# Rotary embedding on one core: rotation in three VectorE operations, and two rows of batch 0 stored early in float32

## The chip, the cores and the metric

The kernel runs on one core of a Trainium2 chip. The metric is device time in microseconds (us), taken from start to end of one execution; lower is better. Runs carry a state (fast or slow); every timed run quoted here is a fast one.

## The reference

The kernel applies a rotary embedding. Each row of 64 numbers is split into two halves of 32, which are rotated against each other by tables of cos and sin that depend on the sequence position only.

```python
# x: (8, 2048, 16, 64) float32; cos, sin: (2048, 32) float32
x1 = x[..., :32]; x2 = x[..., 32:]
out1 = x1 * cos - x2 * sin
out2 = x1 * sin + x2 * cos
return np.concatenate([out1, out2], axis=-1)
```

The input is 67.1 MB and so is the output. There are four multiplications for every pair of numbers moved, so the first thing to ask of any change is whether it moves fewer bytes.

## The kernel before

Each of the 8 batches is one tile `xt` of 128 partitions by 16,384 elements in float16 (16 positions `j`, 16 heads, 64 numbers). GpSimd issues the loads, which cast float32 to float16 on the way, and the stores, which cast back. There are five `xt` buffers. The two tables and the first two positions of batch 0 (`head`) come in float32 through SyncE and are cast on ScalarE.

```python
def rotate(xt):
    v = tmp_pool.tile([P, J, H, D], f16)
    # [...] sin_b, neg_b, cos_b: the float16 tables, broadcast over the heads
    nc.vector.tensor_mul(out=v[:, :, :, 0:Dh], in0=xt[:, :, :, Dh:D], in1=neg_b)   # -x2*sin
    nc.vector.tensor_mul(out=v[:, :, :, Dh:D], in0=xt[:, :, :, 0:Dh], in1=sin_b)   #  x1*sin
    # [...]
    nc.vector.tensor_mul(out=xw, in0=xw, in1=cos_b)                                #  x*cos, in place
    nc.vector.tensor_add(out=xa, in0=xa, in1=v...)                                 #  sum, in place

tiles = [load(b) for b in range(NBUF)]        # five loads issued at the start
# [...] ScalarE: head -> tiles[0], then the tables to float16
for b in range(B):
    rotate(tiles[b])
    if b < B - 1:
        store(b, tiles[b])
    if b + NBUF < B:
        tiles.append(load(b + NBUF))
# [...] the last batch goes out in three parts, the last two positions of it
#       cast by ScalarE and stored in float32 through SyncE
```

## Time and profile before

| | kernel before |
|---|---|
| time, median of 6 runs | 317.51 us (317.43 to 317.98) |
| span of the profiled execution | 315.6 us |
| VectorE busy | 209.2 us, 66% |
| DMA queues' share of 16 engines' span | 98.0% (GpSimd's) and 2.2% (SyncE's) |
| HBM traffic | 67.63 MB read, 67.11 MB written |

First come lines of the page of the kernel before: the span, VectorE's busy time, the DMA busy share in 40 equal slices (tenths, 9 is 90% or more), the two DMA queues, the HBM total, and the first line of the chain of work that ended last (followed back from the last instruction, at each step to what released it). In the profile DVE is VectorE, ACT ScalarE, POOL GpSimd and SP SyncE.

```profile
span 315.6 us, 126 instructions
...
DVE 209.2 (66%) x32; ACT 6.8 (2%) x6; POOL 9.4 (3%) x21
...
DMA  9899999999999999999999999999999999999998
...
q0 software_dynamic: 2448, 99.09, 98.0%
q1 hardware_dynamic: 576, 2.62, 2.2%
HBM read 67.63 MB, written 67.11 MB: 427 GB/s over the span
...
issue 25%; DMA 23%; DVE 21%; another core or an unknown queue 13%; POOL 1%; ACT 1%; SPq 0%; POOLq 0%; DVEq 0%; ACTq 0%
```

The reader should see two things. The DMA engines are at 9 tenths in nearly every slice, and the total, 134.7 MB in 315.6 us, is 427 GB/s. The chain line, on the other hand, gives VectorE 21% of the span, and "issue", time in which the engine waited for nothing that the profile shows, even more. Read alone it suggests that VectorE is worth working on.

Next are groups of VectorE instructions of the kernel before, with shapes kept apart: line, operation, operands, count, then busy us and mean ns of one, then the idle time before them.

```profile
L72 DVE TENSOR_TENSOR xt<-xt,v 128x16384 f16<-128x16384 f16 x8 | 69.5, 8692 | 0.3
L70 DVE TENSOR_TENSOR xt<-xt,cos_h 128x16384 f16<-128x16384 f16 x8 | 69.5, 8692 | 4.2 <-ACT cos_h L81 3.9
L67 DVE TENSOR_TENSOR v<-xt,neg_h 128x8192 f16<-128x8192 f16 x8 | 35.4, 4425 | 50.1 <-DMA xt<-in_x_dram 49.9
L68 DVE TENSOR_TENSOR v<-xt,sin_h 128x8192 f16<-128x8192 f16 x8 | 35.3, 4417 | 0.0
```

The four operations of a batch take 4.42 + 4.42 + 8.69 + 8.69 = 26.2 us. From the two sizes an operation costs about 0.15 us plus 0.52 us for a thousand elements.

Then the timeline of the kernel before: start, duration, instruction, and in brackets what it had waited for. Line 58 issues a store, line 51 a load.

```profile
23.51 4.43 DVE L67 TENSOR_TENSOR v<-xt,neg_h 128x8192 f16<-128x8192 f16 x1 [23.51 <-DMA xt<-in_x_dram]
27.85 4.42 DVE L68 TENSOR_TENSOR v<-xt,sin_h 128x8192 f16<-128x8192 f16 x1
35.55 0.62 ACT L81 CAST cos_h<-cos_f 128x512 f16<-128x512 f32 x1 [17.98 <-DMA cos_f<-in_cos_dram]
36.20 8.69 DVE L70 TENSOR_TENSOR xt<-xt,cos_h 128x16384 f16<-128x16384 f16 x1 [3.93 <-ACT cos_h L81]
...
54.18 0.54 POOL L58 DMA_DIRECT2D out_dram<-xt  x1 [50.14 <-DVE xt L72]
...
121.83 0.53 POOL L51 DMA_DIRECT2D xt<-in_x_dram  x1 [41.14 <-DMA out_dram<-xt]
...
141.13 0.53 POOL L51 DMA_DIRECT2D xt<-in_x_dram  x1 [18.76 <-DMA out_dram<-xt]
...
237.47 4.42 DVE L67 TENSOR_TENSOR v<-xt,neg_h 128x8192 f16<-128x8192 f16 x1 [24.82 <-DMA xt<-in_x_dram]
```

These lines give the transfer rate a second time. Load 5 was issued when store 0 had landed (121.8 us) and load 6 when store 1 had landed (141.1 us), so the one store between them, 8.39 MB, took 19.3 us. Eight loads and eight stores of this size make nearly the whole span. The lines also show how early VectorE is: the first store was issued at 54.2 us and had to wait in the queue behind five loads.

### The profile page before, as it was taken

To read this page: it belongs to the slowest core of one execution; us is meant where nothing else is said; L and a number is where in the kernel's file an instruction comes from. 1 tells how busy PE (TensorE), PEld (TensorE's weight loads), DVE (VectorE), ACT (ScalarE), POOL (GpSimd) and SP (SyncE) were. 2 spreads that over 40 slices of the span, in tenths; PEclk is the share of its full clock that TensorE was granted. 3 is DMA by queue.
4 is the path that set the end of the run, shared out by engine and by line. 5 is a ranking of instruction groups with operands and counts; after the bars stand their busy time and mean duration, and the time that the engine had idled before them with its cause. 6 is when DMAs were issued, how large, how long until landed. Compare 5 with 4: busy or idle time off the path is not lost.

```text
span 315.6 us, 126 instructions
## 1 busy us (share of the span) xinstructions
DVE 209.2 (66%) x32; ACT 6.8 (2%) x6; POOL 9.4 (3%) x21
## 2 busy tenths in 40 slices
DVE  0009599999999999999979999990009994000000
ACT  4010000000000000000000000000000002000000
POOL 3000000000000000010000000100000001000000
DMA  9899999999999999999999999999999999999998
GB/s 278 184 261 207 200 249 216 199 199 249 216 199 266 399 424 507 399 332 233 233 199 199 390 407 399 399 532 266 199 224 507 399 399 498 432 399 399 432 424 341
DMA packets 3024, 101.71 MB, mean 322 GB/s; under 512 B 336, under 2 KB 336, under 8 KB 592
## 3 DMA queue, kind: packets, MB, share of 16 engines
q0 software_dynamic: 2448, 99.09, 98.0%
q1 hardware_dynamic: 576, 2.62, 2.2%
HBM read 67.63 MB, written 67.11 MB: 427 GB/s over the span
## 4 chain that ended last, share of the span: by engine, by line
issue 25%; DMA 23%; DVE 21%; another core or an unknown queue 13%; POOL 1%; ACT 1%; SPq 0%; POOLq 0%; DVEq 0%; ACTq 0%
DMA xt<-in_x_dram 12%; DMA cos_f<-in_cos_dram 11%; DVE xt L70 8%; DVE xt L72 8%; DVE v L68 3%; DVE v L67 1%; ACT head L105 1%; POOL out_dram L58 1%; POOL xt L51 0%; ACT cos_h L81 0%; SPq L45 0%; SPq L36 0%; POOLq L58 0%; DVEq L67 0%
## 5 line engine op out<-in xcount | busy, mean ns | idle before, releaser
L70 DVE TENSOR_TENSOR xt<-xt,cos_h 128x16384 f16<-128x16384 f16 x8 | 69.5, 8692 | 4.2 <-ACT cos_h L81 3.9
L72 DVE TENSOR_TENSOR xt<-xt,v 128x16384 f16<-128x16384 f16 x8 | 69.5, 8692 | 0.3
L67 DVE TENSOR_TENSOR v<-xt,neg_h 128x8192 f16<-128x8192 f16 x8 | 35.4, 4425 | 50.1 <-DMA xt<-in_x_dram 49.9
L68 DVE TENSOR_TENSOR v<-xt,sin_h 128x8192 f16<-128x8192 f16 x8 | 35.3, 4417 | 0.0
L51 POOL DMA_DIRECT2D xt<-in_x_dram x8 | 4.4, 560 | 117.1 <-DMA out_dram<-xt 116.3
L105 ACT CAST head<-xt 128x2048 f32<-128x2048 f16 x1 | 1.9, 1897 | 227.6 <-DVE xt L72 227.6
L58 POOL DMA_DIRECT2D out_dram<-xt x7 | 3.7, 535 | 87.8 <-DVE xt L72 87.8
L95 POOL DMA_DIRECT2D out_dram<-xt x1 | 0.5, 531 | 50.5 <-DVE xt L72 50.5
L75 ACT CAST xt<-head 128x2048 f16<-128x2048 f32 x1 | 1.9, 1898 | 3.4 <-DMA head<-in_x_dram 3.4
L75 ACT ACT_TABLE_LOAD x1 | 1.3, 1283 | 0.7 <-PEq L127 0.7
L81 ACT CAST cos_h<-cos_f 128x512 f16<-128x512 f32 x1 | 0.6, 617 | 18.0 <-DMA cos_f<-in_cos_dram 18.0
L79 ACT CAST sin_h<-sin_f 128x512 f16<-128x512 f32 x1 | 0.6, 617 | 9.1 <-DMA sin_f<-in_sin_dram 9.1
L80 ACT ACTIVATE neg_h<-sin_f 128x512 f16<-128x512 f32 x1 | 0.6, 624 | 0.0
L97 POOL DMA_DIRECT2D out_dram<-xt x1 | 0.5, 531 | 0.0
L127 POOL MEMSET const-float32-0.0<- 128x1 f32 x1 | 0.1, 98 | 0.2 <-issue 0.2
L127 POOL MEMSET const-bfloat16-1.0<- 128x1 bf16 x1 | 0.1, 101 | 0.0
L127 POOL MEMSET const-float32-1.0<- 128x1 f32 x1 | 0.1, 98 | 0.0
L127 POOL MEMSET const-uint8-127<- 128x1 uint8 x1 | 0.1, 98 | 0.0
## 6 DMA issues: line engine op xcount, KB each, us to landing
xt<-in_x_dram POOLq DMA_DIRECT2D x7, 4096.0 KB, 41.1
out_dram<-xt POOLq DMA_DIRECT2D x1, 4608.0 KB, 42.3
xt<-in_x_dram POOLq DMA_DIRECT2D x1, 3584.0 KB, 22.2
out_dram<-xt POOLq DMA_DIRECT2D x1, 2560.0 KB, 47.9
head<-in_x_dram SPq DMA_DIRECT2D x1, 1024.0 KB, 4.7
out_dram<-head SPq DMA_DIRECT2D x1, 1024.0 KB, 8.4
sin_f<-in_sin_dram SPq DMA_DIRECT2D x1, 256.0 KB, 15.2
cos_f<-in_cos_dram SPq DMA_DIRECT2D x1, 256.0 KB, 33.9
```

The lines of the kernel that those rows point to most:

```text
L51: nc.gpsimd.dma_start(out=xt[:, j0:J, :, :].rearrange("p j h d -> p (j h d)"), in_=x[b].rearrange("(p j) h d -> p j (h d)", j=J)[:, j0:J, ...
L58: nc.gpsimd.dma_start(out=out[b].rearrange("(p j) h d -> p (j h d)", j=J), in_=xt)
L67: nc.vector.tensor_mul(out=v[:, :, :, 0:Dh], in0=xt[:, :, :, Dh:D], in1=neg_b)
L68: nc.vector.tensor_mul(out=v[:, :, :, Dh:D], in0=xt[:, :, :, 0:Dh], in1=sin_b)
L70: nc.vector.tensor_mul(out=xw, in0=xw, in1=cos_b)
L72: nc.vector.tensor_add(out=xa, in0=xa, in1=v.rearrange("p j h d -> p (j h d)"))
L75: nc.scalar.copy(out=tiles[0][:, 0:JA, :, :].rearrange("p j h d -> p (j h d)"), in_=head.rearrange("p j h d -> p (j h d)"),)
L79: nc.scalar.copy(out=sin_h, in_=sin_f)
L80: nc.scalar.mul(out=neg_h, in_=sin_f, mul=-1.0)
L81: nc.scalar.copy(out=cos_h, in_=cos_f)
L95: gate = nc.gpsimd.dma_start(out=dst, in_=src)
L105: nc.scalar.copy(out=head.rearrange("p j h d -> p (j h d)"), in_=src)
```

## The change

It has two parts. The two half multiplies become one, which reads the two halves of each row in swapped order against a table that holds minus sin and sin side by side. And the two positions of batch 0 that SyncE loads are rotated on their own, cast to float32 by ScalarE and stored through SyncE early, so that GpSimd's store of batch 0 is 1 MB smaller. The intent is less VectorE work and an earlier start of storing.

```diff
-    sin_h = const_pool.tile([P, J, Dh], f16)
-    neg_h = const_pool.tile([P, J, Dh], f16)
+    sin_h = const_pool.tile([P, J, D], f16)
[...]
-    def rotate(xt):
+    def rotate(xt, j0, j1):
[...]
-        nc.vector.tensor_mul(out=v[:, :, :, 0:Dh], in0=xt[:, :, :, Dh:D], in1=neg_b)
-        nc.vector.tensor_mul(out=v[:, :, :, Dh:D], in0=xt[:, :, :, 0:Dh], in1=sin_b)
+        xe = xt[:, js, :, :].rearrange("p j h (e d) -> p j h e d", e=2)
+        nc.vector.tensor_mul(
+            out=v[:, js, :, :].rearrange("p j h (e d) -> p j h e d", e=2),
+            in0=xe[:, :, :, ::-1, :],
+            in1=sin_b,
+        )
[...]
-    nc.scalar.copy(out=sin_h, in_=sin_f)
-    nc.scalar.mul(out=neg_h, in_=sin_f, mul=-1.0)
+    nc.scalar.copy(out=sin_h[:, :, Dh:D], in_=sin_f)
+    nc.scalar.mul(out=sin_h[:, :, 0:Dh], in_=sin_f, mul=-1.0)
     nc.scalar.copy(out=cos_h, in_=cos_f)
+    rotate(tiles[0], 0, JA)
+    nc.scalar.copy(out=head..., in_=tiles[0][:, 0:JA, :, :]...)
+    nc.sync.dma_start(out=out[0]...[:, 0:JA, :]..., in_=head...)
[...]
-        rotate(tiles[b])
+        rotate(tiles[b], JA if b == 0 else 0, J)
```

GpSimd's store of batch 0 leaves the first two positions out.

More of the change, by code (lines that the diff above doesn't have):

```diff
@@ L57, in store @@
     def store(b, xt):
+        j0 = JA if b == 0 else 0
         nc.gpsimd.dma_start(
-            out=out[b].rearrange("(p j) h d -> p (j h d)", j=J), in_=xt
+            out=out[b].rearrange("(p j) h d -> p j (h d)", j=J)[:, j0:J, :].rearrange("p j f -> p (j f)"),
+            in_=xt[:, j0:J, :, :].rearrange("p j h d -> p (j h d)"),
         )
-    def rotate(xt):
+    def rotate(xt, j0, j1):
         v = tmp_pool.tile([P, J, H, D], f16)
-        sin_b = sin_h.unsqueeze(2).to_broadcast([P, J, H, Dh])
-        neg_b = neg_h.unsqueeze(2).to_broadcast([P, J, H, Dh])
-        cos_b = cos_h.unsqueeze(2).to_broadcast([P, J, 2 * H, Dh])
-        nc.vector.tensor_mul(out=v[:, :, :, 0:Dh], in0=xt[:, :, :, Dh:D], in1=neg_b)
-        nc.vector.tensor_mul(out=v[:, :, :, Dh:D], in0=xt[:, :, :, 0:Dh], in1=sin_b)
-        xw = xt.rearrange("p j h (e d) -> p j (h e) d", d=Dh)
+        n = j1 - j0
+        js = slice(j0, j1)
+        shape = [P, n, H, 2, Dh]
+        sin_b = sin_h[:, js, :].rearrange("p j (e d) -> p j e d", e=2).unsqueeze(2).to_broadcast(shape)
+        cos_b = cos_h[:, js, :].unsqueeze(2).to_broadcast([P, n, 2 * H, Dh])
+        xe = xt[:, js, :, :].rearrange("p j h (e d) -> p j h e d", e=2)
[4 more added lines that the diff above has]
+        )
+        xw = xt[:, js, :, :].rearrange("p j h (e d) -> p j (h e) d", d=Dh)
         nc.vector.tensor_mul(out=xw, in0=xw, in1=cos_b)
-        xa = xt.rearrange("p j h d -> p (j h d)")
-        nc.vector.tensor_add(out=xa, in0=xa, in1=v.rearrange("p j h d -> p (j h d)"))
+        xa = xt[:, js, :, :].rearrange("p j h d -> p (j h d)")
+        nc.vector.tensor_add(out=xa, in0=xa, in1=v[:, js, :, :].rearrange("p j h d -> p (j h d)"))
     tiles = [load(b) for b in range(NBUF)]
@@ L78 @@
     )
-    nc.scalar.copy(out=sin_h, in_=sin_f)
-    nc.scalar.mul(out=neg_h, in_=sin_f, mul=-1.0)
+    nc.scalar.copy(out=sin_h[:, :, Dh:D], in_=sin_f)
+    nc.scalar.mul(out=sin_h[:, :, 0:Dh], in_=sin_f, mul=-1.0)
     nc.scalar.copy(out=cos_h, in_=cos_f)
+    rotate(tiles[0], 0, JA)
+    nc.scalar.copy(
+        out=head.rearrange("p j h d -> p (j h d)"),
+        in_=tiles[0][:, 0:JA, :, :].rearrange("p j h d -> p (j h d)"),
+    )
+    nc.sync.dma_start(
+        out=out[0].rearrange("(p j) h d -> p j (h d)", j=J)[:, 0:JA, :].rearrange("p j f -> p (j f)"),
+        in_=head.rearrange("p j h d -> p (j h d)"),
+    )
     def part(b, j0, j1):
```

## The prediction

> **What bounds the kernel now.** The DMA engines do. The page's slices give DMA 9 tenths nearly throughout, the queue table gives the GpSimd queue 98.0% and the SyncE queue 2.2% of 16 engines' span; VectorE is busy 66%. HBM traffic is 67.63 + 67.11 MB, 427 GB/s over the 315.6 us span. The waits confirm the rate: store 0 landed at 121.8, store 1 at 141.1, so 8.39 MB took 19.3 us; load 5 landed at 160.2, store 2 at 199.1, load 7 at 237.4: 38.2 to 38.9 us per pair. The Trainium skill ("DMA: Bandwidth & Descriptors", Specifications) states a fabric ceiling of 435 GB/s; the trace agrees within 2%. At that rate 134.7 MB need 310 us, so there is nearly nothing to win without moving fewer bytes.
>
> **What the change does.**
> 1. The two half multiplies (4.425 + 4.417 us) become one over 16,384 elements that reads the halves swapped. Innermost step stays 1 and the type float16; the skill ("Vector Engine (DVE) Microarchitecture Reference", table of perf-mode triggers) looks only at the innermost step. So I expect the 8.69 us of the other 16,384-element operations: 0.15 us saved a batch. The page lists negative steps as not measured; no run shows it yet.
> 2. Batch 0 is split: three operations over 2,048 elements (estimate from 8.69 us for 16,384 and 4.42 for 8,192: 1.2 us each) and three over 14,336 (7.6 us each). VectorE's total stays about 209 us.
> 3. VectorE goes in order. The head's second operation waits for cos, ready at 36.2. Before, both multiplies by sin of batch 0 ran at 23.5 to 32.3, ahead of that wait; now the large one stands behind it. Batch 0 ends near 36.2 + 2.4 + 22.9 = 61.5 us, not 53.6. Later batches end near 88, 114, 140, 166, 192, 218 us.
> 4. 1 MB of float32 goes out through SyncE near 40 us; the GpSimd store of batch 0 shrinks by as much. Total bytes are unchanged.
>
> **On the critical path: nothing.** Five loads (41.9 MB) keep the queue full until about 100 us, so store 0 issued at 62 in place of 54 finds the same queue. The early store delays loads 1 to 4 by about 2.4 us and shortens store 0 by as much. Store 3 can be issued at about 141 (GpSimd waits until then before load 6) and its batch is ready at 140; store 5 is ready at 192, needed at 218. Load 7 still lands near 237; VectorE's wait before it absorbs the 8 us (24.8 before, about 19 after), so the tail is the same.
>
> **Predicted time:** 317.4 us, range 316.2 to 319.2. Faster by over 2%: 1%; within 2%: 95%; slower by over 2%: 4%.
>
> **What would show it.** Right: DMA at 9 tenths throughout; the merged multiply at 8.69 us; store 0 issued near 62 us; load 7 landing at 236 to 239; the last batch's wait 18 to 20 us. Wrong at step 1: the merged multiply at about 17 us. Wrong at step 3: store 0 still near 54. Wrong on the path: slices with DMA clearly under 9 tenths between 100 and 300 us, or load 7 landing over 2 us from 237.
>
> **What would make it wrong.** If the swapped read halves VectorE's rate, a batch takes 34.6 us, VectorE becomes the bound, the last batch ends near 310 us and 8.4 MB remain to be stored: about 330 us, slower by 4%. If float32 rows through SyncE cost more engine time than through GpSimd, 1 us is added at most.

## More of the kernel before

The Trainium skill ("DMA: Bandwidth & Descriptors", section "Specifications") states a fabric ceiling of 435 GB/s, and 427 is within 2% of it. The figure agrees, but not the place: the page counts it at the ports of SBUF, where this kernel's batches move as float16, half the bytes that are counted here (see the last section).

## The result, and the profile after

| | before | after |
|---|---|---|
| time, median of 6 runs | 317.51 us (317.43 to 317.98) | 317.85 us (316.94 to 318.75) |
| ratio, 95% interval | | 1.0008 (0.9988 to 1.0028) |
| span of the profiled execution | 315.6 us | 315.2 us |
| VectorE busy | 209.2 us | 209.1 us |

A ratio here and below is the mean time of one kernel's fast runs over that of the other's of the same rounds, so it is not quite the ratio of the medians. The time is the same.

The same page lines of the changed kernel:

```profile
span 315.2 us, 126 instructions
...
DVE 209.1 (66%) x27; ACT 8.7 (3%) x7; POOL 9.4 (3%) x21
...
DMA  9899999999999999999999999999999999999997
...
q0 software_dynamic: 2448, 98.04, 97.2%
q1 hardware_dynamic: 720, 3.67, 3.0%
...
DVE 25%; DMA 21%; issue 18%; another core or an unknown queue 18%; POOL 1%; ACT 1%; SPq 0%; POOLq 0%; ACTq 0%; DVEq 0%
```

The DMA row is still at 9 tenths to the end. The queue shares moved from GpSimd to SyncE by 0.8% of the span with the 1.05 MB that changed sides.

VectorE groups of the changed kernel by shape, the columns as before:

```profile
L71 DVE TENSOR_TENSOR v<-xt,sin_h 128x16384 f16<-128x16384 f16 x7 | 60.8, 8692 | 23.2 <-DMA xt<-in_x_dram 23.0
L79 DVE TENSOR_TENSOR xt<-xt,v 128x16384 f16<-128x16384 f16 x7 | 60.8, 8692 | 0.2
...
L71 DVE TENSOR_TENSOR v<-xt,sin_h 128x14336 f16<-128x14336 f16 x1 | 7.6, 7624 | 0.0
...
L71 DVE TENSOR_TENSOR v<-xt,sin_h 128x2048 f16<-128x2048 f16 x1 | 1.2, 1226 | 13.4 <-ACT sin_h L87 13.4
```

The merged multiply takes 8.692 us, exactly what the other operations of 16,384 elements take. The swapped read costs nothing. The merge saves less than the one fixed part of 0.15 us a batch, though: the two half multiplies had overlapped (the second started at 27.85 us, the first ended at 27.94), and from one batch to the next VectorE now takes 26.18 us (56.94 to 83.12) in place of 26.24 (53.65 to 79.89). VectorE's busy time fell by 0.6 us with the merge alone (below), and the split of batch 0 gives most of that back.

The timeline of the changed kernel, whose line 58 issues a store and line 50 a load:

```profile
30.80 0.62 ACT L88 CAST cos_h<-cos_f 128x512 f16<-128x512 f32 x1 [17.39 <-DMA cos_f<-in_cos_dram]
31.45 1.23 DVE L77 TENSOR_TENSOR xt<-xt,cos_h 128x2048 f16<-128x2048 f16 x1 [16.78 <-ACT cos_h L88]
...
33.97 7.62 DVE L71 TENSOR_TENSOR v<-xt,sin_h 128x14336 f16<-128x14336 f16 x1
...
57.20 0.54 POOL L58 DMA_DIRECT2D out_dram<-xt  x1 [53.17 <-DVE xt L79]
...
121.63 0.53 POOL L50 DMA_DIRECT2D xt<-in_x_dram  x1 [37.71 <-DMA out_dram<-xt]
...
236.99 8.69 DVE L71 TENSOR_TENSOR v<-xt,sin_h 128x16384 f16<-128x16384 f16 x1 [22.95 <-DMA xt<-in_x_dram]
```

Against before: the head's second operation (31.45 us) waits for cos, and the large multiply by sin of batch 0 now stands behind it (33.97 us), where both multiplies had begun at 23.5 and 27.9 us before. The first store therefore comes at 57.2 us, later than the 54.2 us of before, although cos came 4.7 us earlier in this execution. At 121.6 us the two timelines have met again: loads 5, 6 and 7 are issued within 0.5 us of before (at 121.6, 140.9 and 198.6 us against 121.8, 141.1 and 199.1), and the last batch starts at 237.0 us in place of 237.5.

### The profile page after: what moved, and what is told of

Read it like the earlier page. It is cut to its first block, busy times and chain, and to the rows that moved or that the text cites. A ratio compares the mean times of both kernels' runs of the same rounds, so it can differ in the third digit from the quotient of the medians.

```text
span 315.2 us, 126 instructions
## 1 busy us (share of the span) xinstructions
DVE 209.1 (66%) x27; ACT 8.7 (3%) x7; POOL 9.4 (3%) x21
## 4 chain that ended last, share of the span: by engine, by line
DVE 25%; DMA 21%; issue 18%; another core or an unknown queue 18%; POOL 1%; ACT 1%; SPq 0%; POOLq 0%; ACTq 0%; DVEq 0%
DMA xt<-in_x_dram 12%; DMA cos_f<-in_cos_dram 9%; DVE xt L79 8%; DVE xt L77 8%; DVE v L71 8%; ACT head L121 1%; POOL out_dram L58 1%; POOL xt L50 0%; ACT cos_h L88 0%; SPq L44 0%; SPq L36 0%; POOLq L50 0%; POOLq L58 0%; ACTq L121 0%
## 5 line engine op out<-in xcount | busy, mean ns | idle before, releaser
L71 DVE TENSOR_TENSOR v<-xt,sin_h 128x16384 f16<-128x16384 f16 (+2 forms) x9 | 69.7, 7744 | 36.6 <-DMA xt<-in_x_dram 23.0
L77 DVE TENSOR_TENSOR xt<-xt,cos_h 128x16384 f16<-128x16384 f16 (+2 forms) x9 | 69.7, 7744 | 17.1 <-ACT cos_h L88 16.8
L79 DVE TENSOR_TENSOR xt<-xt,v 128x16384 f16<-128x16384 f16 (+2 forms) x9 | 69.7, 7744 | 0.3
L121 ACT CAST head<-xt 128x2048 f32<-128x2048 f16 x1 | 1.9, 1897 | 227.3 <-DVE xt L79 227.3
L90 ACT CAST head<-xt 128x2048 f32<-128x2048 f16 x1 | 1.9, 1898 | 2.6 <-DVE xt L79 2.6
```

The costliest lines, as they stand in the source:

```text
L71: nc.vector.tensor_mul(out=v[:, js, :, :].rearrange("p j h (e d) -> p j h e d", e=2), in0=xe[:, :, :, ::-1, :], in1=sin_b,)
L79: nc.vector.tensor_add(out=xa, in0=xa, in1=v[:, js, :, :].rearrange("p j h d -> p (j h d)"))
L90: nc.scalar.copy(out=head.rearrange("p j h d -> p (j h d)"), in_=tiles[0][:, 0:JA, :, :].rearrange("p j h d -> p (j h d)"),)
L121: nc.scalar.copy(out=head.rearrange("p j h d -> p (j h d)"), in_=src)
```

## The experiments

The main theory is that the DMA engines' bytes set the time and that nothing which the change does on VectorE reaches the end. The rivals are these: two real effects of opposite sign cancel (first rival); a later first store costs time, and the change escaped it by luck (second); rows in float32 through SyncE cost the engines more, hidden by a gain elsewhere (third). All kernels gave correct results except where said.

### The merge alone

```diff
 (against the changed kernel)
-    rotate(tiles[0], 0, JA)        # and the head's cast and SyncE store
-        rotate(tiles[b], JA if b == 0 else 0, J)
+        rotate(tiles[b], 0, J)     # store 0 takes all 16 positions
```

> Only the merged multiply; batch 0 is rotated whole and stored whole. Main theory (the DMA engines bound the time, nothing on VectorE's side reaches the end): ratio to before 1.000 within 0.003; merged multiply 8.69 us; VectorE busy about 208.6 us. First rival (two real effects of opposite sign cancel: the merge gains about 1 us, the early store loses about as much): ratio 0.996 to 0.998 here.

Measured: 317.26 us (317.15 to 317.69, 5 runs) against 317.33 us of before, ratio 1.0002 (0.9989 to 1.0015). VectorE was busy 208.6 us and the first store was issued at 54.7 us. The 0.996 to 0.998 that the first rival wanted lies outside the interval.

### The early store alone

```diff
 (against the changed kernel)
-        nc.vector.tensor_mul(out=v..., in0=xe[:, :, :, ::-1, :], in1=sin_b)
+        nc.vector.tensor_mul(out=v[:, js, :, 0:Dh], in0=xt[:, js, :, Dh:D], in1=neg_b)
+        nc.vector.tensor_mul(out=v[:, js, :, Dh:D], in0=xt[:, js, :, 0:Dh], in1=pos_b)
```

> Only the early float32 store of two rows of batch 0, with the four operations of before. Main theory: ratio to before 1.000 within 0.003; batch 0's GpSimd store issued some us later than 54 without effect. First rival (effects cancel): ratio 1.002 to 1.005 here. The spread of the single runs is watched as well: the changed kernel spread over 1.8 us, the kernel before over 0.55 us; if the early store brings the spread, it shows here and not in the run with the merge alone.

Measured: 317.59 us (317.42 to 318.06, 5 runs) against 317.33 us, ratio 1.0012 (0.9999 to 1.0024). The first store came at 62.3 us, 8 us later than before. The interval holds 1.000 and just reaches into the first rival's 1.002, so a cost of up to 0.8 us is not excluded by this run alone. Together with the run before it, a cancellation of two effects of 1 us each is not what happened: there is no gain of 1 us to cancel (the interval of the merge alone allows 0.4 us at most). The runs spread over 0.64 us.

### Batch 0 delayed by 23 us

```diff
 (against the changed kernel; times=4 for the large part of batch 0, else 1)
-        nc.vector.tensor_mul(out=v..., in0=xe[:, :, :, ::-1, :], in1=sin_b)
+        for _ in range(times):
+            nc.vector.tensor_mul(out=v..., in0=xe[:, :, :, ::-1, :], in1=sin_b)
```

> The changed kernel with the large merged multiply of batch 0 done four times (same result), so that batch 0 and all after it end 22.9 us later, seven times the delay that the change brought. Main theory, by queueing transfers of 19.4 us behind one another: every store still joins a queue that is not empty (the first near 80 us, loads end near 102), so 317 to 319 us, and VectorE's wait before the last batch goes from 23 to about 0. Second rival (a later first store costs time one to one or in part, and the change escaped it by luck): up to 340 us.

Measured: 317.42 us (317.19 to 318.05, 4 runs), ratio to before 1.0010 (0.9995 to 1.0025). Lines of this kernel's timeline:

```profile
85.16 0.54 POOL L58 DMA_DIRECT2D out_dram<-xt  x1 [81.11 <-DVE xt L80]
...
121.99 0.54 POOL L50 DMA_DIRECT2D xt<-in_x_dram  x1 [10.11 <-DMA out_dram<-xt]
...
198.98 0.54 POOL L50 DMA_DIRECT2D xt<-in_x_dram  x1 [34.75 <-DMA out_dram<-xt]
```

The first store was issued at 85.2 us, 31 us later than in the kernel before, and loads 5 and 7 still went out at 122.0 and 199.0 us, as in both kernels. VectorE no longer waited for the last batch. A delay of this size is absorbed (the interval leaves room for 0.8 us), and the second rival is wrong in this range.

### Batch 0 delayed by 53 us

The edit is the same with `times=8`.

> The same multiply eight times: 53.3 us of delay. Main theory, by the same queue: the first store comes at about 111 us, some 8 us after the loads have ended, the second at 137, again 8 us after the first has landed; the queue stays full from there, so about 17.5 us over the changed kernel: 333 to 338 us, with DMA slices visibly under 9 tenths near 105 and 130 us. Theory of no coupling at all: unchanged. Second rival (delay costs one to one): about 371 us.

Measured: 334.87 us (332.58 to 335.14, 4 runs) against 317.33 us, ratio 1.0539 (1.0510 to 1.0567), which is 17.5 us more, as expected. Busy time by stretch of this kernel; the last two columns are the DMA share and GB/s. Packets are booked in lumps, so that the share of a stretch of 5 us can be above 1 (1.29 from 125 to 130 us, in a line left out here):

```profile
core 0: us, DVE busy (x) ACT busy (x) POOL busy (x), PEclk, DMA share, GB/s
...
100.00:105.00 5.00, 4.97 (x2) 0.00 (x0) 0.00 (x0) 1.00 0.49 105
105.00:110.00 5.00, 4.96 (x2) 0.00 (x0) 0.00 (x0) 1.00 0.00 0
110.00:115.00 5.00, 5.00 (x1) 0.00 (x0) 0.00 (x0) 1.00 0.00 0
115.00:120.00 5.00, 4.97 (x2) 0.00 (x0) 0.54 (x1) 1.00 0.86 367
```

Now the queue ran dry: it emptied between 100 and 105 us, and the first store was issued at 115.7 us. The sum came out as expected, but by luck: its parts did not. The first store was later than the expected 111 us, because cos was ready 4.9 us later in this execution than in the profile that the expectation was worked out from. The gap was some 13 us and not 8. The second gap, which was to be 8 us, was only about 2 to 3 us (the last packets of store 0 start between 131.5 and 131.75 us and take some 2.1 us, the next packets start after 136.0), because in this kernel the program order on GpSimd had load 5 ahead of store 1, and it went out as soon as store 0 had landed at 134.8 us. So delay is free as long as the queue has work, and from there costs about what the queue stands idle.

### Every merged multiply done twice

This stands in for a merged multiply at half rate, the risk that the prediction named.

```diff
-        nc.vector.tensor_mul(out=v..., in0=xe[:, :, :, ::-1, :], in1=sin_b)
+        for _ in range(1 if j1 == JA else 2):
+            nc.vector.tensor_mul(out=v..., in0=xe[:, :, :, ::-1, :], in1=sin_b)
```

> The changed kernel with the merged multiply of every batch done twice (same result): 34.8 us of VectorE a batch, as if the swapped read ran at half rate, the case that the prediction named as its main risk. Main theory, by queueing transfers: VectorE falls behind the queue only in the last batches; batch 6 ends near 275, batch 7 near 309, and its stores run after that: 331 to 335 us. A theory in which VectorE never matters: 318.

Measured: 335.48 us (335.20 to 337.76, 4 runs) against 317.85 us, ratio 1.0565 (1.0535 to 1.0595), just above the expected range. (In this and the next three experiments 317.85 us is the time of the kernel before in the same rounds; that it equals the changed kernel's median above is chance.) Its stretches, the columns as above:

```profile
core 0: us, DVE busy (x) ACT busy (x) POOL busy (x), PEclk, DMA share, GB/s
...
295.00:300.00 5.00, 5.00 (x1) 0.00 (x0) 0.00 (x0) 1.00 0.01 0
300.00:305.00 5.00, 4.97 (x2) 0.00 (x0) 0.00 (x0) 1.00 0.00 0
305.00:310.00 5.00, 5.00 (x1) 0.00 (x0) 0.00 (x0) 1.00 0.00 0
310.00:315.00 5.00, 1.25 (x1) 1.90 (x1) 1.05 (x2) 1.00 0.55 236
```

The DMA engines stay full early on (a share of 0.99 from 90 to 100 us), although VectorE takes a third longer for a batch. The loss comes at the end alone: from 295 us the queue has nothing to do until the last batch is rotated at 311 us. VectorE's 26.2 us a batch has room up to about the 38.6 us that load and store of one batch take; what it loses at 34.9 us is that the last batches are still on VectorE when all the other transfers are done.

### One VectorE operation in place of three

The result is wrong: only the multiply by cos is left.

```diff
-        nc.vector.tensor_mul(out=v..., in0=xe[:, :, :, ::-1, :], in1=sin_b)
         nc.vector.tensor_mul(out=xw, in0=xw, in1=cos_b)
-        nc.vector.tensor_add(out=xa, in0=xa, in1=v...)
```

> Wrong result on purpose: of the three VectorE operations only the multiply by cos is left, VectorE busy near 70 us in place of 209. Main theory (DMA bound): 316 to 318 us, ratio to before 0.995 to 1.002. A theory in which VectorE's work is on the path to the end (the chain of waits gives it a quarter of the span): 250 to 300 us.

Measured: 317.52 us (317.07 to 318.52, 4 runs) against 317.85 us, ratio 0.9993 (0.9974 to 1.0013). From this kernel's page:

```profile
DVE 69.5 (22%) x9; ACT 8.7 (3%) x7; POOL 9.3 (3%) x21
...
DMA  9899999999999989999999999999999999999997
```

Two thirds of VectorE's work are gone, 140 us, and the time is the same. This is the plainest proof that the quarter of the span which the chain of waits gives to VectorE is not time that VectorE costs: in this kernel the chain gives VectorE 8% of the span, and the time is the same.

### Half a batch less read

The result is wrong: the second half of batch 7 is not loaded, and what is stored there is batch 6's.

```diff
+        jn = J // 2 if b == B - 1 else J          # load(b) reads j0:jn
-            tiles[b][:, j0:j1, :, :]...
+            tiles[b - 1 if j0 >= J // 2 else b][:, j0:j1, :, :]...
-        rotate(tiles[b], JA if b == 0 else 0, J)
+        rotate(tiles[b], JA if b == 0 else 0, J // 2 if b == B - 1 else J)
-    dst, src = part(B - 1, 0, 9)                  # and 9 -> 8 in the next part
+    dst, src = part(B - 1, 0, 8)
```

> Wrong result on purpose: the second half of the last batch is neither loaded nor rotated, and what is stored there is the second half of batch 6. 4.19 MB less are read, the rest of the traffic is unchanged. Main theory: 4.19 MB at 427 GB/s, 9.8 us less: 307 to 309 us. If the time were bound by VectorE or by waits: 4 us less at most from the halved last rotation, or nothing.

Measured: 307.66 us (307.52 to 308.02, 4 runs) against 317.85 us, ratio 0.9676 (0.9663 to 0.9690): 10.2 us for 4.19 MB, which is 411 GB/s. It halves the last rotation as well, but the run before this one showed that such a cut alone brings nothing. Removing 3% of the bytes does what removing two thirds of VectorE's work did not.

### Two rows of six more batches through SyncE

```diff
     def store(b, xt):
-        j0 = JA if b == 0 else 0
+        j0 = JA
[...]
+        if 0 < b < B - 1:
+            dst, src = part(b, 0, JA)
+            nc.scalar.copy(out=head..., in_=src)
+            nc.sync.dma_start(out=dst, in_=head...)
```

> The changed kernel with the first two rows of batches 1 to 6 stored through SyncE in float32 as well, 6.3 MB more by that way and so much less through GpSimd. Main theory (a byte of float32 on the HBM side costs the engines the same on both ways: in the changed kernel's queue table 1.05 MB moved from 98.0 to 97.2% on one side and from 2.2 to 3.0% on the other): ratio to before 0.997 to 1.004. Third rival (float32 rows through SyncE cost more engine time, up to 1 us for 1 MB, hidden in the change by a gain elsewhere): up to 6 us more, 323 to 324 us.

Measured: 318.03 us (317.97 to 318.14, 5 runs) against 317.85 us, ratio 1.0002 (0.9989 to 1.0014). Seven times as many early rows as the change has cost at most 0.5 us by the interval, where the third rival wanted up to 6 us, so it is wrong. The queue lines of this kernel's page:

```profile
q0 software_dynamic: 2448, 91.75, 92.1%
q1 hardware_dynamic: 1584, 9.96, 22.2%
```

These shares add to 114%. A sum over 100% of the engines' span cannot be engine work alone; when both queues have work, the time of a packet in this view probably includes something else, such as waiting (not tested), so shares of two queues that run together are not what each costs the engines. The argument from 0.8% against 0.8% in the expectation was weaker than it looked; the measured time carries the conclusion.

### The tables through GpSimd, ahead of the loads

This was a try at a kernel that beats both.

```diff
-    nc.sync.dma_start(out=sin_f, in_=sin...)
-    nc.sync.dma_start(out=cos_f, in_=cos...)
+    nc.gpsimd.dma_start(out=sin_s, in_=sin...)    # cast to float16 on the way
+    nc.gpsimd.dma_start(out=cos_h, in_=cos...)
```

> A try at a version that beats both: in the changed kernel the sin and cos tables are loaded through GpSimd with a cast to float16, ahead of the batch loads, in place of float32 through SyncE beside them (DMA share 0.88 to 0.89 from 10 to 20 us in the kernel before, while these small rows were under way). Main theory: VectorE starts batch 0 at its landing near 25 us, the first store is issued near 48 us, and none of that reaches the end; the most that better early slices can give is about 1 us: ratio to before 0.996 to 1.002. Rival (the wait for cos that heads the chain of waits is on the path): 5 to 10 us less.

Measured: 318.67 us (318.17 to 319.12, 5 runs) against 317.56 us, ratio 1.0032 (1.0018 to 1.0046). The expected 0.996 to 1.002 was missed, on the slow side. Lines of its timeline, where the loads are at line 49 and stores at line 57:

```profile
2.44 2.66 POOL L49 DMA_DIRECT2D xt<-in_x_dram  x5
...
50.10 0.54 POOL L57 DMA_DIRECT2D out_dram<-xt  x1 [45.00 <-DVE xt L78]
...
238.72 8.69 DVE L70 TENSOR_TENSOR v<-xt,sin_h 128x16384 f16<-128x16384 f16 x1 [24.90 <-DMA xt<-in_x_dram]
```

The first store was issued at 50.1 us, earlier than in any other kernel with the full rotation, and the kernel was the slowest of those whose work is not inflated. The two table loads take GpSimd's first 1.2 us, so the batch loads are issued at 2.44 us in place of 1.25, and the last load lands 1.2 us later than in the kernel before (238.7 against 237.5 us). That fits a queue that is full from its first transfer on; the run does not separate it from a cost of the cast tables themselves.

### The changed kernel a second time

> The changed kernel unaltered, a second time on one chip, for its spread: its six runs on record spread over 1.8 us (316.94 to 318.75) and those of the kernel before over 0.55 us. If the change brings the spread, five runs spread over more than 1 us while those of before stay within about 0.6. If the spread was the chip's or chance, both are alike. Ratio to before 1.000 within 0.003.

Measured: 317.21 us (317.12 to 317.55, 5 runs) against 317.56 us (317.21 to 317.93, 9 runs), ratio 0.9991 (0.9978 to 1.0003). The spread of 0.43 us is smaller than that of before on the same chip, so nothing here ties the 1.8 us of the first six runs to the change. What made it was not looked for. cos was ready at 33.6 us here (start of its cast) and the first store came at 60.0 us.

## Why the prediction was right or wrong

- **The bound.** Right. Taking away bytes shortened the time by 10.2 us for 4.19 MB; taking away 140 us of VectorE work did nothing.
- **Step 1, the merged multiply.** Right in its duration: 8.692 us, as long as the other operations of 16,384 elements. The saving of 0.15 us a batch was mis-sized: it was 0.06 us (26.24 to 26.18 us), because the two half multiplies had overlapped by 0.09 us. Neither figure reaches the end of the kernel. The Trainium skill ("Vector Engine (DVE) Microarchitecture Reference", section 5.1 on performance modes) makes the two-element rate depend, among the steps, on the innermost one and lists how an operand with a negative step streams among what was not measured. Here the negative step is that of the dimension above the innermost, and it cost nothing.
- **Step 2, the sizes of the split.** Right: 1.226 and 7.624 us against the estimates of 1.2 and 7.6; VectorE 209.1 us in all.
- **Step 3, the order on VectorE.** The mechanism was right, the size not in the profiled run: the first store came at 57.2 us, not 62, and VectorE's wait before the last batch was 23.0 us, not 18 to 20. The term that was off is when cos is ready. It was taken as 36.2 us from one profile, and it varies from run to run with the same code: its cast began at 30.8 us in the profile after, at 33.6 in the second run of the same kernel, and at 35.8 with the early store alone, where the first store came at 62.3 us as forecast.
- **Step 4, the early store.** Right, in that bytes only change sides. The limit of 1 us put on a dearer SyncE path, for which the prediction gives no working, was generous: seven such stores cost at most 0.5 us.
- **Nothing on the critical path.** Right. The delay of 23 us shows that even a multiple of the change's delay is absorbed, and the delay of 53 us shows that it is no longer so when the first store misses the end of the five loads at about 102 us. A first store at 85.2 us was free and one at 115.7 us was not; where between them the limit lies was not tested. The change moved the first store by 3 to 8 us, to 62.3 us at the latest, so some 23 us at least were to spare.
- **What would make it wrong.** The case of half rate was put at about 330 us, and doing the multiply twice gave 335.5. The last batch ended at 311.3 and not 310 us, the transfers after it took 22.1 us to the end of the span and not 19, and the measured time is about 2 us above the span, which the estimate left out. Nothing here hung on it.

What stays open: with the early store alone the interval reached 1.0024, so a cost of some tenths of a microsecond can be neither shown nor excluded. That the transfers set the time is shown; which part of their way (HBM, the DMA engines or the ports between) holds them at 427 GB/s is not.

## What to carry to other kernels

Before costing a change on a compute engine, ask whether the transfers are at their measured rate in every stage. If they are, as here, look at the bytes (4.19 MB less took 10.2 us off), at gaps in the queue (the delay of 53 us), and at what stands behind the last load (every multiply done twice); and a chain of waits that names a compute engine does not say otherwise. A compute engine that is off the bound has a slack that can be estimated from the queue: here the five loads ended at about 102 us, and a first store at 85.2 us cost nothing. Splitting work so that a small part can start early may put the large part behind the small part's wait, as the wait for cos did here; here it cost nothing because such slack was there.

## What the Trainium skill lacked or had wrong

- "DMA: Bandwidth & Descriptors", section "Where 436 GB/s comes from", says without a condition that for transfers between HBM and SBUF the HBM side, about 358 GB/s per core, binds. With one core in use the runs show 427 GB/s of HBM traffic over the whole span of the kernel before. The condition stands elsewhere on the page: its section "Measured" gives 425 GB/s for a single core and about 358 for each with both streaming. The runs agree with the first; the second was not tested.
- The same page puts its ceiling of 435 GB/s at the ports of SBUF and does not say which side of a casting transfer counts. By the stretches of the delayed kernel, casting loads brought 210 GB/s of float16 into SBUF at a DMA share of 0.97, which is 420 GB/s of float32; by the timelines a batch of 8.39 MB of float32 takes 19.3 us as a store and 19.1 as load 5 (141.1 to 160.2 us). So the float32 side counts, at about 435 GB/s (8.39 MB in 19.3 us), with half of that at SBUF. Storing 6.3 MB more as float32 on both sides, through SyncE, doubled their bytes at SBUF and changed nothing (ratio 1.0002).
- The same page describes the turns that queues take on an engine, but gives no time for a small transfer beside a full queue. The 256 KB of cos, issued at 1.6 us, were ready between 30.8 and 36.1 us (start of its cast).
- "Vector Engine (DVE) Microarchitecture Reference", section 5.1, lists an operand with a negative step as not measured. With a step of minus 32 elements in the second innermost dimension and rows of 32 float16 elements, 16,384 elements took 8.692 us, the same as without it.
